# Experts' token rows sorted by indirect writes to memory, and one pool of five PSUM banks in the attention

## The chip, the cores and the metric

One core of a Trainium2 chip runs the whole program once. The metric is the device time of one execution in microseconds (us); a kernel's time is the median of its runs.

## What is computed

Two blocks on 256 tokens of width 1024, batch 1, in float32. The first block is two layers of a hybrid mixer and a SwiGLU feed-forward network. The second block takes its result as `x`, and a context `s` of another 256 tokens, through two layers that each end in a hierarchical mixture of experts; layer 0 mixes by pooling, layer 1 by attention from the tokens to context and tokens. The context is updated in layer 0 only, so layer 0's experts serve 512 tokens and layer 1's 256.

```python
x = first_block(x, ...)                      # 2 x (hybrid mixer, SwiGLU), final norm
for i in range(DEPTH):                       # second block: pool layer, attention layer
    a_lat = modulate(x, norm1_g[i], sh1, sc1)
    ...
    x = x + g1 * y_lat
    x = x + g2 * hier_moe(modulate(x, norm2_g[i], sh2, sc2), ...)
    if ctx_upd:                              # i == 0
        s = s + cg1 * y_ctx
        s = s + cg2 * hier_moe(modulate(s, norm2_g[i], csh2, csc2), ...)

def hier_moe(h, w_rg, b_rg, w_re, b_re, w_gate, w_up, w_down):
    # the best of 4 groups, its best 2 of 4 experts: 2 of 16 experts for a token
    gates = jnp.sum(jax.nn.one_hot(expert_id, N_EXPERTS) * e_w[..., None], axis=1)
    a = jnp.einsum('nd,edf->nef', hf, w_gate)          # 1024 -> 256
    b = jnp.einsum('nd,edf->nef', hf, w_up)
    hid = jax.nn.silu(a) * b * gates[..., None]
    return jnp.einsum('nef,efd->nd', hid, w_down)      # 256 -> 1024

def block(q_blk):                            # attention: 16 query heads, 4 key heads, 512 keys
    s = jnp.einsum('bqhgd,bkhd->bhgqk', q_blk, k_all)
    p = jax.nn.softmax(s, axis=-1)
    return jnp.einsum('bhgqk,bkhd->bqhgd', p, v_all)
```

## The kernel before

**Products.** A float32 product of the accuracy wanted is made of three fast ones (`fp32r`): each factor is split into a high part, which ScalarE writes (L422, L463), and a low rest, which VectorE or now and then GpSimd subtracts (L425, L465, L467); then hi x hi, hi x lo and lo x hi are added in one PSUM bank (L457 to L459). Weights come through SP's queue in loads of 1 MB into three buffers (`stg`, L406), and are split half by half into four pairs of buffers (`whi`, `wlo`), in layer 0's experts into three more (`xhi`, `xlo`: `wx`, every third split).

**Order.** The program is one long list of instructions with tiles from pools; the framework orders each engine's instructions ahead of time by a modelled timeline with the program's order as priority, takes buffers from the pools, and sets the semaphores. On the chip each engine, and each of the queues of SP and GpSimd, works its list in that fixed order.

**Stages in the order of time.** Mixer and feed-forward of layer 0, then of layer 1 of the first block. The second block's conditioning weights (`w_mod`, 80 loads of 0.5 MB through GpSimd's queue, used at L1268) run in between. While the second feed-forward network works, `context` (L1487) takes the context tokens through the pool layer, a step behind every few products, and writes their split rows to memory (`tokd`, L1527). Then `latent` (L1533) does the same for the tokens, and `experts0` (L1710) runs layer 0's experts for both. Then come the attention (`attn`), layer 1's tokens and experts, and the output.

**Sorting tokens for experts.** `tokens` (L1428) normalizes 256 tokens, makes the router's logits, and hands the rows on in four groups of 256 columns to a `sink`, which splits them (L1525, L1556). `route` (L1573) finds each token's two experts and its place among an expert's tokens (`pm`). In its second half it makes the row number `si` = 128 x expert + 64 x segment + place in a table of 16 x 128 rows; segment 0 are the tokens, 1 the context; if an expert has more than 64 tokens of a segment, another path is taken (`every_expert`). `quad_all` (L1757) does four experts at a time. First it builds a 0/1 matrix per segment (`places`, L1707) and multiplies the tokens' split rows with it, so that the tokens come out sorted by expert and transposed: 16 steps of four matmuls of 256 columns (L1768), each evacuated by ScalarE, every fourth by VectorE (L1770). Then, expert by expert, 24 matmuls of 512 columns with gate and up weights (L1781 to L1783), the activation (L1785 to L1787), two transposes (L1790) with a split, 12 matmuls with the down weights (L1798 to L1800), and a write of the 128 x 1024 result rows to `eb` (L1804). `gather` (L1733) fetches each token's two result rows by `si` with indirect DMAs, and `combine` weighs and adds them.

**Attention's banks.** `pools_b` (L1211) gives the attention two PSUM banks for projections (`mm`), three for scores (`ms`), two for transposes and others (`mx`), one for the outputs. In a step of `heads` two banks of scores are made (L2000, L2001), their maxima taken on VectorE (L2003), exponentials on ScalarE (L2007), the results transposed (L2011), evacuated, and multiplied with the values (L2016). The projections of the next heads are issued between.

Of the kernel before, what the change touches and what calls it, by code (L numbers as in the profile page):

```python
# [8 lines left out]
F32 = mybir.dt.float32  # L9
F32R = mybir.dt.float32r  # L10
# [9 lines left out]
KT = 8  # L20
# [243 lines left out]
class Halves:  # L264
# [3 lines left out]

    def __getitem__(self, key):
        return self.t[key[1] // 4][key[0], key[1] % 4]  # L270


class Prog:
# [926 lines left out]
    def pools_m(self, ctx):  # L1200

        P = self.pools(ctx)
        self.a1 = P("a1m", 4)
        self.pmm = P("pmm3", 3, space=PSUM)
        self.pm1 = P("pm1", 1, space=PSUM)
        self.pmx = P("pmx3", 4, space=PSUM)
        self.wx = P("wx", 3)
        self.b8 = P("b8", 3)
        self.b4 = P("b4", 2)

    def pools_b(self, ctx):  # L1211

        P = self.pools(ctx)
        self.a1 = P("a1b", 8)
        self.cb = P("cb", 1)
        self.a2 = P("a2d", 12)
        self.b8 = P("b8b", 8)
        self.b4 = P("b4b", 5)
        self.pmm = P("pmm4", 2, space=PSUM)
        self.pmx = P("pmx4", 2, space=PSUM)  # L1220
        self.pms = P("pms", 3, space=PSUM)
        self.pmo = P("pmo", 1, space=PSUM)
        self.c.update(self.consts("c2", self.cb))

# [81 lines left out]
            sink(kt, t, sh[:, kt:kt + 1])  # L1306

    def ms(self):
        return self.pms.tile([128, 512], F32, tag="ms", name="ms")

    def e8(self, dt=F32):
        return self.b8.tile([128, 8, 256], dt, tag="b8", name="b8")
# [115 lines left out]
    def tokens(self, x, l, seg, per, hold, SH, sink):  # L1428
# [44 lines left out]
        route = self.route(l, lg, seg, per)  # L1473
        self.R[l, seg] = next(route)
        yield
        for g, ps in enumerate(held):
            h = self.t2()
            for i in range(2):
                e = nc.vector.scalar_tensor_tensor(h[:, i], ps[:, i], r[:, i:i + 1], SH[:, g * 256:g * 256 + 256], op0=ALU.mult,
                                                   op1=ALU.add)  # L1480
                if seg == 0 and g + i == 0:
                    self.tc.keep_in_program_order(e)
            sink(g, h)
            yield
        next(route)

    def context(self):  # L1487

# [33 lines left out]

        def sink(g, ps):
            hi, lo = self.t2(F32R), self.t2(F32R)
            self.split_act(ps, hi, lo)  # L1525
            for w, z in enumerate((hi, lo)):
                nc.gpsimd.dma_start(self.tokd[w].rearrange("p (i n) -> p i n", i=2)[:, :, g * 256:g * 256 + 256], z)  # L1527
        yield from self.tokens(xc, 0, 1, 128, self.mx, SH, sink)
# [4 lines left out]
    def latent(self, x):  # L1533
# [19 lines left out]

        def sink(g, ps):
            s = slice(g * 256, g * 256 + 256)
            self.split_act(ps, self.tok[0][0][:, :, s], self.tok[0][1][:, :, s])  # L1556
        yield from self.tokens(x, 0, 0, 128, self.hold, SH, sink)

    def first(self, w, prio, tag):
# [150 lines left out]
    def experts0(self, R):  # L1710

        nc = self.nc
        for quad in range(4):
            self.quad_all(0, quad, self.tok, [self.places(r, quad) for r in R])
        with self.tc.If(self.count(R) > 64):
            Y = self.every_expert(0, self.tok, R)
            for seg, r in enumerate(R):
# [39 lines left out]
    def quad_all(self, l, quad, tok, Dt):  # L1757

        nc, a = self.nc, self.a
        X = [self.b8.tile([128, 4, 4, 2, 2, 64], F32R, tag="b8", name="xg") for hf in range(2)]  # L1760
        order = [(k, seg) for k in range(KT) for seg in range(2)]
        if quad == 0:
            order.sort(key=lambda o: -o[1])
        for n, (k, seg) in enumerate(order):
            ps = self.mm()
            for w in range(2):
                for t in range(2):
                    nc.tensor.matmul(ps[:, w], tok[seg][w][:, t, k * 128:k * 128 + 128],  # L1768
                                     Dt[seg][:, t].rearrange("p e s -> p (e s)"), start=t == 0, stop=t == 1)
            (nc.vector.tensor_copy if k % 4 == 3 else nc.scalar.copy)(  # L1770
                X[k // 4][:, k % 4, :, :, seg].rearrange("p e w s -> p w e s"), ps.rearrange("p w (e s) -> p w e s", e=4))
        for el in range(4):
            e = 4 * quad + el
            ps = self.mm().rearrange("p a b -> p (a b)")
            for c in range(2):
                for hf, (hi, lo) in enumerate(self.halves(a["moe"][l, e, c], 1024)):
                    for kk in range(2):
                        k = c * 4 + hf * 2 + kk
                        xh, xl = (X[c][:, hf * 2 + kk, el, w].rearrange("p g s -> p (g s)") for w in range(2))
                        s = slice(kk * 512, kk * 512 + 512)  # L1780
                        nc.tensor.matmul(ps, xh, hi[:, s], start=k == 0, stop=False)  # L1781
                        nc.tensor.matmul(ps, xh, lo[:, s], start=False, stop=False)
                        nc.tensor.matmul(ps, xl, hi[:, s], start=False, stop=k == KT - 1)  # L1783
# [18 lines left out]
            for q in range(2):  # L1802
                nc.scalar.copy(eo[:, q * 512:q * 512 + 512], po[q])
            (nc.sync if e == 15 else nc.gpsimd).dma_start(self.eb[e * 128:e * 128 + 128, :], eo)  # L1804

    def quad_few(self, l, quad, tok, D, gate, g2r, y):

# [329 lines left out]
    def rows_behind(self):  # L2137
# [4 lines left out]
        self.eb = self.dr.tile([2560, 1024], F32, name="eb")  # L2142
        for t in range(4):
            nc.gpsimd.dma_start(self.eb[2048 + t * 128:2176 + t * 128, :], z)

    def run(self):
        from contextlib import ExitStack
# [59 lines left out]
```

## Time and profile before

| | |
|---|---|
| Median of 3 runs | 1731.03 us (1719.16 to 1735.97) |
| The profiled execution | 1719.79 us, of it 1718.0 us from its first to its last instruction (the span) |
| Busy share of the span | TensorE 96%, VectorE 62%, ScalarE 47%, GpSimd 11% |
| DMA | 359.73 MB, on average 209 GB/s |
| Layer 0's experts | about 1184 to 1361 us |
| Attention's heads | about 1452 to 1542 us |

Times in the rows are us from the span's start. PE is TensorE's matmuls, PEld its weight loads (which overlap them), DVE VectorE, ACT ScalarE, POOL GpSimd, SPq the queue of SP. `out<-in` are the program's tiles; x is a count. The end of a matmul is modelled and consecutive ones overlap, so what a matmul costs is read from start to start. The DMA share is the mean busy share of the core's 16 DMA engines; the granted clock is TensorE's, as a share of the full one.

### The profile page before, as it was taken

Reading aid. Unit: us, or ns where it says so; the run is one execution under the profiler, and the core shown is the slowest. Engines: PE = TensorE matmul, PEld = TensorE weight load, DVE = VectorE, ACT = ScalarE, POOL = GpSimd, SP = SyncE. Lnnn points to the kernel's source line nnn. Section 1 sums busy time; section 2 is a strip of 40 time slices with the busy share of each in tenths; the row PEclk is TensorE's granted clock in tenths of the full one; section 3 lists DMA queues with packets and bytes.
Section 4 is the critical chain, followed back from the end, with each engine's and each line's share of the span. In section 5 each row is a group of like instructions: output and inputs, shape, how many; then the busy total and the mean of one; then the engine's idle time right before and its main releaser. Section 6 shows DMA issues by size and latency. Waiting matters only on the chain. (4 is left out here: it accounts for less than half of the span.)

```text
span 1718.0 us, 29620 instructions
## 1 busy us (share of the span) xinstructions
PE 1648.1 (96%) x12089; PEld 1403.2 (82%) x12089; DVE 1070.9 (62%) x1946; ACT 805.0 (47%) x1260; POOL 181.1 (11%) x281
## 2 busy tenths in 40 slices
PE   7999999999999999999999999998999799888997
PEld 6977889999999886788999999966777599566453
DVE  6863575666665595357677778457777567555222
ACT  4633264344444373235455554335777644552121
POOL 4311000110000230101002111020000201000000
PEclk9999999999999999999999999997999989998999
DMA  8574248875555665335555558565888744118991
GB/s 323 175 256 148 96 161 282 296 244 176 192 176 180 241 210 202 124 123 209 196 173 188 184 194 259 180 224 202 320 319 310 292 160 123 31 31 318 398 405 55
DMA packets 67276, 359.73 MB, mean 209 GB/s; under 512 B 8040, under 2 KB 13080, under 8 KB 34744
## 3 DMA queue, kind: packets, MB, share of 16 engines
q1 hardware_dynamic: 41280, 279.86, 45.0%
q0 software_dynamic: 25632, 77.47, 13.4%
q8 instruction: 100, 1.64, 0.4%
q10 hardware_dynamic: 216, 0.37, 0.1%
q14 instruction: 48, 0.39, 0.1%
HBM read 339.76 MB, written 14.71 MB: 206 GB/s over the span
## 5 line engine op out<-in xcount | busy, mean ns | idle before, releaser
L425 DVE TENSOR_TENSOR wlo<-stg,whi 128x1024 fp32r<-128x1024 f32 (+1 forms) x379 | 462.3, 1226 | 286.9 <-ACT whi L422 279.6
L422 ACT ACTIVATE whi<-stg 128x1024 fp32r<-128x1024 f32 (+1 forms) x383 | 402.2, 1056 | 475.8 <-PE mm L458 289.2
L457 PE MATMUL mm<-hh,whi 128*128 128x256 f32 x1408 | 408.3, 290 | 10.9 <-ACT whi L422 9.7
L458 PE MATMUL mm<-hl,whi 128*128 128x256 f32 x1408 | 403.1, 286 | 0.0
L459 PE MATMUL mm<-hh,wlo 128*128 128x256 f32 x1408 | 402.4, 286 | 0.6 <-DVE wlo L425 0.5
L457 PEld LDWEIGHTS mm<-hh,whi 128*128 128x128 f32 x1408 | 271.9, 193 | 22.7 <-ACT whi L422 9.7
L459 PEld LDWEIGHTS mm<-hh,wlo 128*128 128x128 f32 x1408 | 272.0, 193 | 3.9 <-issue 2.5
L458 PEld LDWEIGHTS mm<-hl,whi 128*128 128x128 f32 x1408 | 272.1, 193 | 3.3 <-issue 2.9
L411 POOL DMA_DIRECT2D st<-in_w_mod x80 | 42.6, 534 | 416.1 <-PE ad L1268 371.8
L494 POOL TENSOR_TENSOR a<-a,a 128x256 f32<-128x256 f32 x30 | 27.5, 918 | 312.1 <-ACT a L492 310.9
L614 PE MATMUL mm<-wlo,hh 128*128 128x512 f32 (+1 forms) x160 | 60.0, 375 | 0.0
L615 PE MATMUL mm<-whi,hl 128*128 128x512 f32 (+1 forms) x160 | 60.0, 375 | 0.0
L613 PE MATMUL mm<-whi,hh 128*128 128x512 f32 (+1 forms) x160 | 59.5, 378 | 0.0
L1268 PE MATMUL ad<-st,sc 128*32 128x256 f32 x640 | 51.8, 389 | 2.9 <-DMA st<-in_w_mod 2.9
L457 PE MATMUL mm<-lg,whi 128*128 128x256 f32 x192 | 54.5, 284 | 0.0
L457 PE MATMUL mx<-lg,whi 128*128 128x256 f32 x192 | 54.4, 285 | 0.0
L458 PE MATMUL mm<-lg,whi 128*128 128x256 f32 x192 | 54.3, 283 | 0.0
L459 PE MATMUL mm<-lg,wlo 128*128 128x256 f32 x192 | 54.3, 283 | 0.0
L458 PE MATMUL mx<-lg,whi 128*128 128x256 f32 x192 | 54.2, 283 | 0.0
L459 PE MATMUL mx<-lg,wlo 128*128 128x256 f32 x192 | 54.1, 283 | 0.0
L1862 DVE TENSOR_TENSOR eo<-mx,g2r 128x512 f32<-128x512 f32 x16 | 11.0, 690 | 66.1 <-PE mx L1857 65.8
L425 DVE TENSOR_TENSOR xlo<-stg,xhi 128x1024 fp32r<-128x1024 f32 x31 | 37.8, 1220 | 13.9 <-ACT xhi L422 13.9
(600 smaller groups left out, 3597.1 us busy)
## 6 DMA issues: line engine op xcount, KB each, us to landing
stg<-in_moe SPq DMA_DIRECT2D x57, 1024.0 KB
stg<-in_w_gu SPq DMA_DIRECT2D x44, 1024.0 KB
stg<-in_w_fm SPq DMA_DIRECT2D x43, 1024.0 KB
st<-in_w_mod POOLq DMA_DIRECT2D x80, 512.0 KB, 5.5
w<-in_moe SPq DMA_DIRECT2D x27, 1024.0 KB
stg<-in_w_dn SPq DMA_DIRECT2D x22, 1024.0 KB
stg<-in_w_tm SPq DMA_DIRECT2D x16, 1024.0 KB
stg<-in_w_br SPq DMA_DIRECT2D x12, 1024.0 KB
```

The lines of the kernel that those rows point to most:

```text
L411: self.nc.gpsimd.dma_start(t, src)
L422: nc.scalar.activation(hi[:, :n], t, AF.Copy)
L425: (nc.gpsimd if pool else nc.vector).tensor_sub(lo[:, :n], t, hi[:, :n])
L457: nc.tensor.matmul(out, hi, xh, start=first and k == 0, stop=False)
L458: nc.tensor.matmul(out, hi, xl, start=False, stop=False)
L459: nc.tensor.matmul(out, lo, xh, start=False, stop=last and k == n - 1)
L494: self.adder.tensor_add(sq[0][1], sq[0][1], s)
L613: nc.tensor.matmul(ps[i], xh[:, ts], hi[:, s], start=first, stop=False)
L614: nc.tensor.matmul(ps[i], xh[:, ts], lo[:, s], start=False, stop=False)
L615: nc.tensor.matmul(ps[i], xl[:, ts], hi[:, s], start=False, stop=last)
L1268: nc.tensor.matmul(ps[32 * n:32 * n + 32, :256], self.sc[:, 2 * q + hf], ws[hf][:, n * 256:n * 256 + 256], start=hf == first, stop=hf == last)
L1862: nc.vector.tensor_mul(eo, po[q], g2r[:, q * 512:q * 512 + 512])
```

## The change

- `tokens` gets, for layer 0, two row tiles of 128 x 1024 (`rowsof`) instead of four tiles of 128 x 2 x 256, so that each token's whole row lies in one partition. Behind the last group four indirect DMAs on GpSimd's queue write the rows (128 at a time, for each of a token's two experts) to the rows `si` of a new table `xs` of 2048 x 1024 in memory. For the context the second half of `route` comes ahead of the rows and not behind them. The two sinks split the rows in halves of 256 columns instead of 512.
- `quad_all` keeps the matmul dispatch for quad 0. For quads 1 to 3 a new `slots` loads, for each expert, its 128 rows from `xs` through SP's queue into one of two buffers (`xr`), transposes them in eight steps of 128 columns into two banks, and splits each bank (512 columns) once on ScalarE and VectorE. The 0/1 matrices of these quads are not built.
- `rows_behind` also clears rows 512 to 2047 of `xs`: 12 writes of 0.5 MB through GpSimd's queue.
- The third `wx` buffer pair makes room for the `xr` buffers.
- In the attention the banks for projections and scores become one pool of five under one tag.

```diff
+class Pieces(list):
+
+    def __getitem__(self, key):
+        return list.__getitem__(self, key[1])
...
-        self.wx = P("wx", 3)
+        self.wx = P("wx", 2)
+        self.xr = P("xr", 2)
...
-        self.pmm = P("pmm4", 2, space=PSUM)
+        self.pmm = P("pmm4", 5, space=PSUM)
         self.pmx = P("pmx4", 2, space=PSUM)
-        self.pms = P("pms", 3, space=PSUM)
...
     def ms(self):
-        return self.pms.tile([128, 512], F32, tag="ms", name="ms")
+        return self.pmm.tile([128, 512], F32, tag="mm", name="ms")
...
         self.R[l, seg] = next(route)
         yield
+        if seg:
+            next(route)
+        H = l == 0 and [self.rowsof(seg) for i in range(2)]
         for g, ps in enumerate(held):
-            h = self.t2()
+            h = Pieces([z[:, g * 256:g * 256 + 256] for z in H]) if H else self.t2()
...
-        next(route)
+        if not seg:
+            next(route)
+        if H:
+
+            for i in range(2):
+                for k in range(2):
+                    nc.gpsimd.indirect_dma_start(
+                        out=self.xs[:, :], out_offset=bass.IndirectOffsetOnAxis(ap=self.R[l, seg]["si"][:, k, i, 0:1], axis=0),
+                        in_=H[i], in_offset=None)
+
+    def rowsof(self, seg):
+        return self.t4().rearrange("p a b -> p (a b)") if seg else self.ca.tile([128, 1024], F32, tag="row", name="row", bufs=2)
...
-            self.split_act(ps, hi, lo)
+            for i in range(2):
+                self.split_act(ps[:, i], hi[:, i], lo[:, i])
...
-            self.split_act(ps, self.tok[0][0][:, :, s], self.tok[0][1][:, :, s])
+            for i in range(2):
+                self.split_act(ps[:, i], self.tok[0][0][:, i, s], self.tok[0][1][:, i, s])
...
-            self.quad_all(0, quad, self.tok, [self.places(r, quad) for r in R])
+            self.quad_all(0, quad, self.tok, [] if quad else [self.places(r, quad) for r in R])
...
+        if quad:
+            pieces = self.slots(quad)
+        else:
+            X = [self.b8.tile([128, 4, 4, 2, 2, 64], F32R, tag="b8", name="xg") for hf in range(2)]
...
         for el in range(4):
             e = 4 * quad + el
+            piece = next(pieces)
...
-                        xh, xl = (X[c][:, hf * 2 + kk, el, w].rearrange("p g s -> p (g s)") for w in range(2))
+                        xh, xl = (piece(k, w) for w in range(2))
...
+    def slots(self, quad):
+
+        nc = self.nc
+        for el in range(4):
+            e = 4 * quad + el
+            if el % 2 == 0:
+                X = self.b8.tile([128, 2, KT, 2, 128], F32R, tag="b8", name="xg")
+            r = self.xr.tile([128, 1024], F32, tag="xr", name="xr")
+            nc.sync.dma_start(r, self.xs[e * 128:e * 128 + 128, :])
+            for q in range(2):
+                ps = self.mm().rearrange("p a (k s) -> p (a k) s", k=2)
+                for k in range(4):
+                    nc.tensor.transpose(ps[:, k], r[:, (4 * q + k) * 128:(4 * q + k) * 128 + 128], self.idf)
+                x = X[:, el % 2, 4 * q:4 * q + 4]
+                self.split_act(ps, x[:, :, 0], x[:, :, 1])
+            yield lambda k, w, x=X[:, el % 2]: x[:, k, w]
...
+        self.xs = self.dr.tile([2048, 1024], F32, name="xs")
+        for t in range(4, 16):
+            nc.gpsimd.dma_start(self.xs[t * 128:t * 128 + 128, :], z)
```

## Rows read from the trace of the kernel before

**Rows 1.** The page: span, and busy time of TensorE with instructions.

```profile
span 1718.0 us, 29620 instructions
PE 1648.1 (96%) x12089; PEld 1403.2 (82%) x12089; DVE 1070.9 (62%) x1946; ACT 805.0 (47%) x1260; POOL 181.1 (11%) x281
```

**Rows 2.** Windows: length, busy us of five engines, clock, DMA share, GB/s.

```profile
1180.00:1190.00 10.00, 9.78 (x60) 8.63 (x59) 7.95 (x10) 8.52 (x12) 0.00 (x0) 1.00 0.27 95
1190.00:1352.00 162.00, 151.86 (x743) 122.95 (x742) 125.28 (x146) 123.54 (x180) 7.46 (x14) 1.00 0.89 324
1240.00:1250.00 10.00, 9.32 (x43) 6.96 (x42) 8.09 (x10) 8.62 (x12) 0.53 (x1) 1.00 0.93 345
1325.00:1330.00 5.00, 3.86 (x16) 2.67 (x15) 4.31 (x6) 4.04 (x5) 0.53 (x1) 1.00 0.63 206
1600.00:1650.00 50.00, 50.00 (x260) 26.32 (x260) 12.18 (x25) 11.14 (x23) 0.00 (x0) 1.00 1.01 406
```

**Rows 3.** Timeline of TensorE: transposes of experts 11, 12 and 13.

```profile
1315.64 0.38 PE L1790 MATMUL mx<-idf,a 128*128 128x128 f32 x2
1333.74 0.38 PE L1790 MATMUL mx<-idf,a 128*128 128x128 f32 x2
1341.09 0.38 PE L1790 MATMUL mx<-idf,a 128*128 128x128 f32 x2
```

**Rows 4.** Waits, 1184-1361 us: total, times, longest; ScalarE, load queue.

```profile
ACT xhi L422 <- DMA stg<-in_moe: 22.9, 9, 4.1
SPq L406 <- DVE wlo L425: 54.9, 15, 9.2
```

**Rows 5.** Groups of 1184 to 1361 us: busy us, mean ns, idle before.

```profile
L1768 PE MATMUL mm<-Dt,tok 128*128 128x256 f32 x198 | 30.3, 290 | 2.3 <-ACT xg L1770 2.3
L1770 ACT CAST xg<-mm 128x512 fp32r<-128x512 f32 x37 | 21.2, 607 | 0.3 <-PE mm L1783 0.3
L1770 DVE CAST xg<-mm 128x512 fp32r<-128x512 f32 x13 | 8.9, 686 | 2.4 <-PE mm L1768 2.4
L1707 DVE TENSOR_TENSOR Dt<-cst_cg,pm 128x512 fp32r<-128x512 f32 x5 | 3.4, 681 | 0.0
```

**Rows 6.** Timeline of TensorE: start, length, one merged run each.

```profile
1222.54 0.38 PE L1790 MATMUL mx<-idf,a 128*128 128x128 f32 x2
1222.68 1.84 PE L1768 MATMUL mm<-Dt,tok 128*128 128x256 f32 x12
1225.28 1.11 PE L1768 MATMUL mm<-Dt,tok 128*128 128x256 f32 x8
1226.23 0.63 PE L1800 MATMUL mx<-xhi,a 128*128 128x512 f32 x2
```

**Rows 7.** Groups: subtractions of 512 columns (1100-1184 us), 256 (1184-1361 us).

```profile
L465 DVE TENSOR_TENSOR tok<-a,tok 128x512 fp32r<-128x512 f32 x4 | 2.6, 681 | 0.0
L467 DVE SCALAR_TENSOR_TENSOR a<-mx,a 128x256 fp32r<-128x256 f32 x16 | 6.7, 417 | 1.4 <-ACT a L463 1.4
```

**Rows 8.** The indirect gathers: issue on GpSimd, and landing.

```profile
L1733 POOL DMA_INDIRECT rows<-eb,si x8: 945/958/1963, 1365.5 to 1374.8; - x8
DMA to landing us min/median/max: 7.9/8.0/10.0
```

**Rows 9.** Timeline of GpSimd: idle time in brackets.

```profile
349.21 0.95 POOL L494 TENSOR_TENSOR a<-a,a 128x256 f32<-128x256 f32 x1 [25.12 <-ACT a L492]
1115.03 2.39 POOL L425 TENSOR_TENSOR wlo<-stg,whi 128x1024 fp32r<-128x1024 f32 x1 [67.14 <-ACT whi L422]
```

**Rows 10.** Window of the clears, and their DMA issues with median landing.

```profile
324.00:364.00 40.00, 40.00 (x347) 39.11 (x346) 32.36 (x40) 20.49 (x31) 6.01 (x9) 1.00 0.68 246
eb<-a POOLq DMA_DIRECT2D x4, 512.0 KB, 11.1
```

**Rows 11.** Attention's heads: window, and TensorE's longest wait in it.

```profile
1452.00:1542.00 90.00, 80.48 (x479) 53.47 (x478) 50.75 (x110) 52.50 (x108) 6.29 (x8) 0.96 0.15 44
PE mx L2011 <- ACT a L2007: 6.2, 6, 1.6
```

More of the change, by code (lines that the diff above doesn't have):

```diff
@@ L1759, in quad_all @@
         nc, a = self.nc, self.a
[L1760 to L1771, printed above, removed]
+        if quad:
+            pieces = self.slots(quad)
+        else:
+            X = [self.b8.tile([128, 4, 4, 2, 2, 64], F32R, tag="b8", name="xg") for hf in range(2)]
+            order = sorted([(k, seg) for k in range(KT) for seg in range(2)], key=lambda o: -o[1])
+            for n, (k, seg) in enumerate(order):
+                ps = self.mm()
+                for w in range(2):
+                    for t in range(2):
+                        nc.tensor.matmul(ps[:, w], tok[seg][w][:, t, k * 128:k * 128 + 128],
+                                         Dt[seg][:, t].rearrange("p e s -> p (e s)"), start=t == 0, stop=t == 1)
+                (nc.vector.tensor_copy if k % 4 == 3 else nc.scalar.copy)(
+                    X[k // 4][:, k % 4, :, :, seg].rearrange("p e w s -> p w e s"), ps.rearrange("p w (e s) -> p w e s", e=4))
+            pieces = (lambda k, w, el=el: X[k // 4][:, k % 4, el, w].rearrange("p g s -> p (g s)") for el in range(4))
         for el in range(4):
             e = 4 * quad + el
+            piece = next(pieces)
             ps = self.mm().rearrange("p a b -> p (a b)")
```

## Prediction

> **What bounds it now.** The page's busy table comes first [rows 1]: in a span of 1718.0 us TensorE is counted busy for 96%. That looks like a kernel in which every matmul taken out is time gained, and the change takes matmuls out. A share over the whole span says nothing of one stage, so the second view is the windows over the stage that the change rewrites, layer 0's sixteen experts [rows 2]. From 1190 to 1352 us TensorE is busy 151.9 of 162 us, and the DMA engines at the same time 89%, moving 324 GB/s: 52.5 MB. Two resources are near their end together there, and the reader should keep both in sight. Third, the order in time [rows 3]: the transposes of the expert before a quad's boundary and of the one behind it are 18.1 us apart (1315.64 to 1333.74), those of two experts inside the quad 7.35 us. One of three is shown; the others take 17.3 and 18.8 us. The extra time is the dispatch: the sixteen products of token rows with 0/1 matrices that sort the next quad's tokens. While TensorE works on it, no split weight is used up, the split buffers and then the three weight buffers stay full, and the loads stop: behind the boundary, from 1325 to 1330 us, the DMA share is 0.63 although weights are still to come [rows 2]. Fourth, the waits [rows 4]: in this stage ScalarE's splits wait for weights that have not landed (22.9 us at one of the two buffer kinds), and the load queue waits mostly for the split that gives a buffer back. So the stage goes back and forth between a dispatch that stops the loads and loads that are then late.
>
> **What the dispatch costs and what takes its place.** Quads 1 to 3 lose 3 x 64 = 192 matmuls of 256 columns (198 in [rows 5], which counts the last six of quad 0). Eight of them in a row take from 1225.28 to 1226.23 us, 0.119 us each [rows 6]: 22.8 us of TensorE. Added are 12 experts x 8 transposes of 128 columns. The expert's own pair of transposes takes from 1222.54 to 1222.68, 0.07 us each [rows 6]; 0.12 us, a dispatch matmul of twice the columns, is the other end. I take 0.09: 8.6 us (6.7 to 11.5). TensorE's need falls by 14.2 us, to 137.7 us in that stretch.
>
> ScalarE loses 36 evacuations of 0.607 us (21.8 us) and gets 24 splits of the same 512 columns (14.6 us): 7 us less. VectorE loses 12 of 0.686 us and six comparisons of 0.681 us that built the 0/1 matrices (12.3 us) and gets 24 subtractions of 0.681 us (16.3 us) [rows 5, 7]: 4 us more. Both were under 80% busy in the stretch (123.5 and 125.3 of 162 us [rows 2]), so neither sets its end.
>
> The DMA engines get more to do: 12 reads of 0.524 MB, 6.3 MB. Two of the row buffers can be filled before 1190 us, where only 95 GB/s move [rows 2], so 52.5 + 6.3 - 1.0 = 57.8 MB are left for the stretch. The rate decides. 324 GB/s at a share of 0.89 are 364 GB/s at a full one. 345 GB/s is what a single stretch without a pause reached (1240 to 1250 us, share 0.93), and 406 GB/s the layer-1 experts' stage, where hardly anything is split [rows 2]. At 364 the bytes need 159 us, at 345 they need 168, at 406 they need 142 and TensorE with the 10 us of gaps that it has now (148 us) would be the limit. I take 364, the row of the same weights on the same queue with the same splits beside them, and another microsecond from the smoother order: the stage gets **4 us shorter**; ends 14 shorter and 6 longer. The 14 us that TensorE gives back are for the most part taken up by the new reads.
>
> A rule of the Trainium skill reads otherwise. SBUF — State Buffer, Summary: rules for kernel authors, says to reckon with about 358 GB/s between HBM and SBUF. By it the bytes would need 161 us and the stage would gain 1 us; the 406 GB/s of layer 1 lie above it, so this trace does not bear it out as a ceiling.
>
> **The split buffers.** One pair of the seven split buffers goes (wx from 3 to 2) to make room for the rows. Six halves are one whole expert, so a step ahead remains. From nothing to a doubling of what TensorE idles in the stretch now (10 us); I take **+1 us**, since the dispatch that emptied and filled these buffers in turns is gone.
>
> **The scatters.** Eight indirect writes replace the sorting matmuls. GpSimd spent 0.96 us (1.96 at most) on one indirect gather and it landed in 8.0 us, 10.0 at most [rows 8]. The context's four come while the feed-forward layer runs: GpSimd then stood idle for 67 us [rows 9]. The latent's four come right before the stage, 4 x 1.0 + 10 = 14 us, and their rows are first read for expert 4, behind four experts of at least 7.35 us each [rows 3]. Both cost nothing as long as the first read of rows does not stand in SP's queue ahead of weights while it waits for the scatter; that would cost the weights behind it a few us once. Taken at 0, the end +3.
>
> The tokens' split goes from four pieces of 512 columns to eight of 256. On VectorE that is 8 x 0.417 in place of 4 x 0.681 us [rows 7], +0.6 us on the path to the first dispatch; the context's is covered by the feed-forward layer. **+0.5 us**.
>
> **The clearing of the sorted rows** is 12 writes of 0.5 MB behind the four that are there, at the start of layer 0's feed-forward. GpSimd's issues cost it 6.4 us out of an idle time of 25 us [rows 9]. The engines are at 0.68 from 324 to 364 us [rows 10], so 0.32 x 40 us x 364 GB/s = 4.7 MB fit in and 1.6 MB, 4.4 us of transfers, are pushed past it, ahead of conditioning weights on the same GpSimd queue which TensorE uses in order. The four writes took 11.1 us to land [rows 10]. Ends 0 and +5; I take **+1 us**.
>
> **The attention's banks.** The heads' stretch, 1452 to 1542 us, has TensorE busy for 80.5 of 90 us, and the named wait is that of the transposes for ScalarE's exponentials, 6.2 us [rows 11]. Scores are made in pairs, and three banks hold one pair and a half, so the second score of the next step must wait until a bank of this step has been exponentiated. Five hold two pairs and leave one for a projection. What can be won ends at the idle 9.5 us. It could cost as well: a projection that comes while four banks hold scores has one bank instead of two of its own, and TensorE's order is fixed, so what stands behind a product that lacks its bank waits too; no row prices it, and I bound it by half of the wait that is there, +3. I take somewhat less than two thirds of the named wait: **-4 us** (-9.5 to +3).
>
> **Sum.** -4 + 1 + 0 + 0.5 + 1 - 4 = -5.5 us on 1718.0, so 1712.5 us of span; 1.8 us lie around it (the profiled execution took 1719.8). The median of the runs, 1731.0, stands 11.2 us above that execution, and I take the same distance for the changed kernel: 1712.5 + 1.8 + 11.2 = **1725.5 us**, written as 1725.
>
> **Rivals.**
> - **Faster: the loads keep up.** With the dispatch gone nothing stops the loads, and they run at layer 1's 406 GB/s. Then TensorE's 148 us set the stretch, the stage gains 14 us, and the time is 1715 us. For it: 406 GB/s at a share of 1.01. Against: in that stage VectorE works 24% of the time, here 77% [rows 2]. HBM Reference in the Trainium skill, Specifications (TRN2), gives about 425 GB/s for a core that streams alone; that speaks for this rival, and no stretch of the experts' stage here shows it.
> - **Slower: the buffers, not the engines, set the rate.** If three weight buffers and six split pairs turn over no faster than now, the loads stay at the stage's 324 GB/s. 57.8 MB then need 178 us, 16 us more than the 162: with the other terms 1745 us. It decides from 357 GB/s downwards, where 57.8 MB need over 162 us. For it: the load queue's waits are for splits [rows 4]. Against: the largest cause that kept the buffers full goes, and the row reads have buffers of their own.
> - **A draw: reads eat the whole gain.** At the unbroken 345 GB/s the stretch is 6 us longer, and if the banks bring nothing too (softmax is a chain through three engines, and more banks shorten none of its steps), the sum is +6 + 1 + 0.5 + 1 = +8.5: 1739 us.
>
> **Chances and range.** Forecast 0.42, loads keep up 0.26, draw 0.18, buffers set the rate 0.14. About 1% (17 us) is what a measurement of this kernel can tell from no change. Faster by more means below 1714: half of the keep-up case (0.13) and a third of the forecast's spread, where the banks bring their whole 9.5 us (0.14). Slower by more means above 1748: the better part of the buffer case (0.09) and a third of the draw, with the clears and the split buffers at their upper ends (0.06). That gives 0.27, 0.58, 0.15. The range runs from the keep-up case with the banks' upper end (1709) a little down, to the buffer case: 1706 to 1745. The forecast's own range is 1714 to 1735.
>
> **What would show it.** In the experts' stretch: no 18 us steps at quad boundaries but even ones near 11 us; TensorE down by about 14 us busy and idle more; the DMA share at 0.95 or more without the dips to 0.6, near 360 GB/s; ScalarE's waits for weights longer than now. If the share stays at 0.89 with the load queue waiting for splits, the buffer case is right; if GB/s go over 395 and TensorE is above 95% busy, the keep-up case. In the heads' stretch the wait for the exponentials should fall from 6.2 to about 2 us. At 361 to 384 us TensorE should show no wait for conditioning weights beyond a few us; a longer one would make the clears the mis-sized term, and a wait of the load queue for the scatter ahead of expert 4 would make it the scatters.

## The result, and the profile after

The changed kernel takes 1747.3 us (median of 4 runs, 1743.4 to 1750.7) against 1726.8 us of the kernel before, measured beside it (median of 4 runs): a ratio of 1.0111, 95% interval 1.0075 to 1.0147. A second set of runs (after_again, below) gave 1.0150 (1.0115 to 1.0185). The profiled execution's span is 1747.5 us against 1718.0 [rows 1].

The profile page of the kernel after, span and busy times:

```profile
span 1747.5 us, 29487 instructions
PE 1646.5 (94%) x11993; PEld 1397.1 (80%) x11993; DVE 1076.4 (62%) x1960; ACT 802.2 (46%) x1256; POOL 196.8 (11%) x301
```

TensorE is busy as long as before, with 96 matmuls fewer by the profile page's count, in a span 29.5 us longer. (Line numbers in a view are those of its own kernel: L1791 is L1768 of the kernel before.) Its timeline at the start of the experts has the largest piece: one idle stretch of 18.87 us, in brackets with what ended it, inside quad 0's dispatch, ahead of 48 of its 64 matmuls.

```profile
1192.58 8.17 PE L1791 MATMUL mm<-Dt,tok 128*128 128x256 f32 x48 [18.87 <-ACT xg L1793]
```

ScalarE and VectorE, which had to evacuate that dispatch, waited in turn, for the transfers that scatter the latent's rows:

```profile
1191.88 0.69 DVE L1793 CAST xg<-mm 128x512 fp32r<-128x512 f32 x1 [9.12 <-DMA xs<-row,si]
...
1191.94 1.56 ACT L1793 CAST xg<-mm 128x512 fp32r<-128x512 f32 x3 [10.44 <-DMA xs<-row,si]
```

And GpSimd issued the four scatters one at a time, each behind the landing of the one before:

```profile
1172.92 1.03 POOL L1500 DMA_INDIRECT xs<-row,si  x1 [1.52 <-DVE si L1651]
1181.30 0.98 POOL L1500 DMA_INDIRECT xs<-row,si  x1 [7.36 <-DMA xs<-row,si]
1184.90 0.96 POOL L1500 DMA_INDIRECT xs<-row,si  x1 [2.62 <-DMA xs<-row,si]
1188.48 0.96 POOL L1500 DMA_INDIRECT xs<-row,si  x1 [2.62 <-DMA xs<-row,si]
```

Nothing in the computation ties quad 0's sorted tokens to the scatters. Memory does: the allocation puts the latent's two row tiles at bytes 204,768 to 212,960 of each partition, in a pool (`ca`) that begins at 196,576, and lays the pool of the sorted tiles (`b8`), 171,744 to 220,896, over them. The evacuations that waited write the first sorted tile, at 171,744 to 188,128, which shares no byte with the rows; only the second, at 204,512 to 220,896, does. So the wait goes with the whole pool: its first writers wait until the last scatter has read its rows.

The queue of SP, which the prediction had named, waited too. The first row read stood there for 19.6 us, with the weights behind it:

```profile
SPq L1839 <- DMA xs<-row,si: 19.6, 1, 19.6
```

Windows of the kernel after (columns as in [rows 2]): the clears' stretch, and the experts' with the same distances to the first gate and the last down matmul as there.

```profile
324.00:364.00 40.00, 40.00 (x346) 39.11 (x346) 30.19 (x38) 20.46 (x30) 10.53 (x20) 1.00 1.01 405
...
1206.00:1378.00 172.00, 149.59 (x667) 116.57 (x666) 131.63 (x156) 120.59 (x169) 7.55 (x14) 0.97 0.91 335
```

The clears fill the idle 32% of the engines [rows 10] and TensorE stays busy for all 40 us. In the experts' stretch 57.6 MB move at 335 GB/s, where 52.5 MB moved at 324 before [rows 2]: 172 us for 162. The waits there, 1200 to 1387 us (total, times, longest), beside [rows 4]:

```profile
ACT whi L428 <- DMA stg<-in_moe: 14.9, 13, 4.3
...
PE mx L1815 <- DVE a L1812: 10.9, 6, 2.7
PE mm L1806 <- ACT whi L428: 9.5, 5, 3.1
ACT xhi L428 <- DMA stg<-in_moe: 9.2, 5, 3.0
...
SPq L412 <- DVE wlo L431: 65.2, 20, 11.4
...
SPq L1839 <- PE mm L1843: 22.6, 8, 4.7
```

The last is the row reads, waiting for a row buffer with the weights behind them; the second is new too, TensorE waiting for an expert's activation, which the dispatch matmuls used to cover. ScalarE's waits for weights are 24.1 us at both kinds of buffer, where they were 35.0 before (22.9 in [rows 4] and 12.1 at the other kind).

### The profile page after: what moved, and what is told of

Its sections match the earlier page's. It is cut to its first block, busy times and chain, and to the rows that moved or that the text cites. A ratio compares the mean times of both kernels' runs of the same rounds, so it can differ in the third digit from the quotient of the medians.

```text
span 1747.5 us, 29487 instructions
## 1 busy us (share of the span) xinstructions
PE 1646.5 (94%) x11993; PEld 1397.1 (80%) x11993; DVE 1076.4 (62%) x1960; ACT 802.2 (46%) x1256; POOL 196.8 (11%) x301
## 5 line engine op out<-in xcount | busy, mean ns | idle before, releaser
L1904 DVE TENSOR_TENSOR eo<-mx,g2r 128x512 f32<-128x512 f32 x16 | 11.1, 692 | 66.1 <-PE mx L1899 65.8
```

Of the source, the lines that this page charges most:

```text
L1904: nc.vector.tensor_mul(eo, po[q], g2r[:, q * 512:q * 512 + 512])
```

## The experiments

The table gives each kernel's median in us and its ratio to before on the same chip, and from the views of single lines **a**, the time from the start of the last conditioning matmul to that of the first gate matmul, and **b**, from there to the start of the last down matmul. Before stood between 1721.8 and 1723.8 us in the sets of the experiments. The last conditioning matmul starts between 1161 and 1175 us in these executions, a shift that a and b leave out. They come from one execution of each kernel: after and after_again, the same kernel, differ by 5.4 us in b, so a smaller difference in a single trace shows little.

| kernel | us | ratio (95%) | a | b | a+b |
|---|---|---|---|---|---|
| before | - | 1 | 17.9 | 175.8 | 193.7 |
| after | 1747.3 | 1.0111 (1.0075-1.0147) | 36.6 | 184.9 | 221.5 |
| row_late | 1743.7 | 1.0109 (1.0072-1.0145) | 15.8 | 193.9 | 209.7 |
| row_late_gp | 1743.1 | 1.0102 (1.0055-1.0150) | 15.9 | 201.1 | 217.0 |
| row_late_one | 1730.7 | 1.0039 (1.0008-1.0069) | 15.8 | 182.4 | 198.2 |
| five_alone | 1729.3 | 1.0043 (1.0014-1.0073) | 17.9 | 176.8 | 194.7 |
| row_clear | 1738.3 | 1.0085 (1.0059-1.0110) | 16.1 | 192.6 | 208.7 |
| row_clear_banks23 | 1734.2 | 1.0075 (1.0048-1.0103) | 17.4 | 184.0 | 201.4 |
| reads_alone | 1727.9 | 1.0042 (1.0015-1.0069) | 17.6 | 186.8 | 204.4 |
| wx2_alone | 1719.1 | 0.9976 (0.9957-0.9996) | 18.1 | 175.2 | 193.3 |
| scatters_alone | 1733.0 | 1.0056 (1.0034-1.0077) | 16.0 | 190.5 | 206.5 |
| row_clear_23_one | 1725.0 | 0.9994 (0.9969-1.0019) | 16.1 | 182.3 | 198.4 |
| wx2_stage4 | 1717.1 | 0.9962 (0.9942-0.9982) | 18.1 | 169.0 | 187.1 |
| scatters_apart | 1728.4 | 1.0035 (1.0014-1.0056) | 17.4 | 178.7 | 196.1 |
| rows_apart | 1730.9 | 1.0045 (1.0022-1.0069) | 16.3 | 185.3 | 201.6 |
| rows_apart_one | 1720.0 | 0.9981 (0.9962-1.0000) | 16.2 | 178.6 | 194.8 |
| rows_apart_gp | 1729.2 | 1.0035 (1.0011-1.0059) | 16.3 | 183.0 | 199.3 |
| apart_five | 1729.8 | 1.0028 (1.0008-1.0048) | 16.2 | 182.6 | 198.8 |
| after_again | 1747.8 | 1.0150 (1.0115-1.0185) | 36.6 | 179.5 | 216.1 |
| wx1_stage5 | 1758.0 | 1.0200 (1.0169-1.0231) | 18.2 | 204.8 | 223.0 |

**The first four: move the memory, move the queue, leave reads out, the banks alone.**

```
 # row_late, in pools_m
-wx, xr, b8, b4
+b8, b4, xr, wx
 # row_late_gp, besides: nc.gpsimd.dma_start(r, self.xs[...]) for nc.sync
 # row_late_one, besides: only "if el == 0:" reads a row tile
 # five_alone: before, with pmm4 of 5 banks and pms gone
```

> The changed kernel with the order of four pools turned round (b8, b4, xr, wx for wx, xr, b8, b4), so that the memory of the latent's two row tiles is given next to the result tiles (b4) and the row buffers (xr) and no longer to quad 0's sorted tiles (xg in b8). Theory (18 us of the loss is the wait of quad 0's evacuations for memory that the scatters still read): TensorE no longer idles 18.9 us ahead of quad 0's products, the first gate matmul comes at about 1182 us and not at 1200.6, and the time falls by 15 to 19 us against the changed kernel, to about 1729 us. Rival (the scatters themselves hold the stage up, by their traffic or by the queue they stand in): the first gate matmul stays near 1200 and the time within 4 us of the changed kernel's.

> As row_late, and the twelve reads of sorted rows go through GpSimd's queue instead of SP's. Theory A (the experts' stretch, 9 us longer than before, is bound by the bytes): the same as row_late within 3 us. Theory B (a row read that waits for its buffer stands ahead of weight loads in SP's queue, 22.6 us in all): 5 to 9 us faster than row_late, and SP's waits for the row buffers are gone. Theory C (one split buffer pair fewer): the same as row_late.

> As row_late, but only the first of a quad's four row blocks is read, and all four experts of the quad are given it: nine of twelve reads (4.7 MB) are left out, so experts 5 to 7, 9 to 11 and 13 to 15 compute with another expert's rows. Theory A (bytes): 4.7 MB at 335 to 368 GB/s are 13 to 14 us of transfers; the stretch gets 8 to 12 us shorter than in row_late. Theory B (row reads ahead of weights in SP's queue): 5 to 8 us shorter here and in row_late_gp alike. Theory C (split buffers): within 3 us of row_late.

> The kernel before with the attention's pool of five banks alone. Forecast's step: 4 us faster than the kernel before (0 to 9.5), the wait of the transposes for the exponentials falls from 6.2 to about 2 us. Rival (softmax is a chain through three engines, and more banks shorten none of its steps): within 2 us of the kernel before; the wait moves to the products with the values.

The stall in quad 0's dispatch went (a: 36.6 to 15.8 us), and the kernel was hardly faster where 15 to 19 us were expected, because other tiles now lay on the rows. Timelines of TensorE and ScalarE in row_late:

```profile
1210.27 1.22 PE L1823 MATMUL mx<-xhi,a 128*128 128x512 f32 x2 [12.05 <-ACT xhi L428]
...
1209.16 2.00 ACT L428 ACTIVATE xhi<-stg 128x1024 fp32r<-128x1024 f32 x2 [4.47 <-DMA xs<-row,si]
```

The split buffers begin at byte 212,704 there, 256 bytes inside the second row tile. Reading from the other queue won nothing. Leaving out 4.7 MB of reads (and with them the right rows) won 11.5 us of a+b, of which 4.9 us are a shorter stall (7.16 us for 12.05). five_alone missed both of its cases: it is 0.43% slower, where the forecast had 4 us less and the rival no more than 2 us either way.

**Rows clear of both, and two parts alone.** row_clear puts a gap of 256 bytes ahead of the split buffers; row_clear_banks23 also takes the pool of five back.

```
 # row_clear
+self.gap = P("gap", 1); nc.gpsimd.memset(self.gap.tile([128, 64], F32, name="gap"), 0.0)
 self.wx = P("wx", 2)
 # reads_alone: before with wx 2 and xr 2, and for quads 1 to 3, ahead of each expert
+nc.sync.dma_start(self.xr.tile([128, 1024], F32, tag="xr", name="xr"), self.eb[2048 + e % 4 * 128:2176 + e % 4 * 128, :])
 # wx2_alone: before with wx 2
```

> The changed kernel with its SBUF laid out so that the latent's two row tiles share bytes with the row-read buffers and the output tiles alone, and no byte with the sorted tiles or with the split buffers (those start 256 bytes further up). Theory M (both stalls at the experts' start, 18.9 us before the gate matmuls in the changed kernel and 12.1 us behind the first of them in row_late, are waits for the memory that the scatters read): no TensorE wait over 3 us between 1180 and 1215 ends with the scatters or behind them, last conditioning to first gate matmul 16 to 18 us, first gate to last down matmul about 182 us (row_late: 193.9), and the kernel at 1729 to 1734. Rival S (the scatters themselves hold up the loads on the DMA engines, whatever the memory): the first gate to last down stretch stays at 190 us or more and the kernel at 1740 to 1746.

> row_clear with the attention's banks as before the change (two for projections, three for scores). If the pool of five is worth the 4 us that the prediction gave it, this is 3 to 5 us slower than row_clear, from the scores' first matmul to the last pv matmul. If five_alone was right (about 4 to 5 us slower behind the gather), it is 3 to 6 us faster than row_clear, and at 1724 to 1729 level with the kernel before.

> The kernel before with two split buffers for three, and twelve reads of 0.5 MB, one ahead of the weights of each expert from 4 to 15, into two buffers that nothing reads (rows of zeros from memory; computes the same). No scatter, no transposes of rows, no splits, and the dispatch matmuls stay. Theory A (the experts' stretch is set by the bytes, at 52.5 MB plus 6.3 MB): first gate to last down matmul 8 to 13 us longer than in wx2_alone, the DMA rate of the stretch up by under 10 GB/s. Rival C (the stretch has 11% of idle DMA time that takes the reads, and the changed kernel's 9 us come from TensorE's order, where no dispatch matmuls cover the activation, and from the waits for splits): within 2 us of wx2_alone, the DMA share up to 0.97 or more.

> The kernel before with two split buffers for three in the experts' stretch, nothing else. The prediction put this at +1 us. If the buffers set the rate of the weights' stream: first gate to last down matmul 4 us or more longer, with longer waits of SP's queue for the VectorE's low parts (54.9 us before). If not: within 2 us.

wx2_alone came out as "not the rate", and 2.7 us better rather than worse. reads_alone did what theory A said of the time: 6.3 MB that nobody uses cost 11.6 us of b, and 8.9 us of the median; the rate rose by 13 GB/s, where under 10 were expected. Windows of b in wx2_alone, then in reads_alone:

```profile
1186.10:1361.30 175.20, 165.59 (x801) 136.59 (x800) 135.74 (x157) 132.25 (x191) 8.00 (x15) 0.98 0.82 303
```

```profile
1181.10:1367.90 186.80, 169.62 (x801) 136.64 (x801) 136.31 (x158) 134.11 (x192) 7.99 (x15) 0.97 0.83 316
```

The share hardly moves, 0.82 to 0.83. At 364 GB/s, a share of 1, the reads need 17.3 us, so the idle 18% took in a third of them; the rest of it was no room. row_clear fits neither theory whole: its a is that of M, its b of 192.6 us that of S, its median lies between the two, and TensorE has no wait of 3 us or more at the experts' start. row_clear_banks23 is 4.1 us faster, which the runs cannot tell from nothing (the intervals overlap), and not level with before. In b, row_clear runs the same sequence of instructions as row_clear_banks23 and took 8.6 us longer; TensorE was busy 163.0 and 157.5 us on it. (The execution of row_clear_banks23 that was profiled, 1725.6 us, is the fastest of its six.) Their timelines behind the same wait, row_clear first:

```profile
1227.05 0.69 PE L1817 MATMUL mx<-idf,a 128*128 128x128 f32 x2 [5.59 <-DVE a L1814]
...
1231.79 0.63 PE L1827 MATMUL mx<-whi,a 128*128 128x512 f32 x1
1232.21 0.63 PE L1825 MATMUL mx<-whi,a 128*128 128x512 f32 x1
1232.64 0.63 PE L1826 MATMUL mx<-wlo,a 128*128 128x512 f32 x1
```

```profile
1219.83 0.44 PE L1818 MATMUL mx<-idf,a 128*128 128x128 f32 x2 [3.80 <-DVE a L1815]
...
1224.12 0.39 PE L1828 MATMUL mx<-whi,a 128*128 128x512 f32 x1
1224.34 0.39 PE L1826 MATMUL mx<-whi,a 128*128 128x512 f32 x1
1224.57 0.39 PE L1827 MATMUL mx<-wlo,a 128*128 128x512 f32 x1
```

Starts 0.43 us apart are the lower of the clock's two levels (1.2 GHz; the granted clock reads 0.50 from 1229.5 to 1233 us in row_clear), 0.23 us the higher (2.4 GHz; 1.00 from 1224.3 to 1230 us in row_clear_banks23). The first still ran at the lower 5 us behind the gap, the second no longer after 4.3. Here a gap cost more than its length.

**Sorting without its use, chain or bytes, one load buffer more.**

```
 # scatters_alone: row_clear_banks23, quads 1 to 3 dispatched as before the change, xs never read
 # row_clear_23_one: row_clear_banks23 with "if el == 0:" ahead of the row read
 # wx2_stage4: before with wx 2, and in load():
+fourth = self.wx and self.nld % 4 == 0
+t = (self.sx if fourth else self.stg).tile([128, 2048], F32, ...)
```

> Sorting without its use: the tokens' halves, the clears and the eight scatters stay as in row_clear, with the rows' memory apart from what the experts' first steps write, but the sorted rows are never read, and all four groups of experts are dispatched by matmuls as before the change (two split buffers, attention's banks as before). The prediction put the scatters at 0 (end +3). Theory A: once their memory is apart they cost nothing, so last conditioning to first gate matmul 16 to 18 us, first gate to last down matmul within 2 us of wx2_alone's 175.2, the kernel within 3 us of wx2_alone (0.997 to 1.000 of before). Rival S (the scatters' 2 MB in packets of one row, and GpSimd's time for them, hold up the loads at the experts' start): first gate to last down 179 us or more and the kernel 4 us or more above wx2_alone, which would explain why row_clear_banks23 stands above reads_alone.

> row_clear_banks23 with one row read for every four: the experts of a group read the first one's tile again, so nine of twelve reads (4.7 MB) are left out, and with them the right rows; every transpose, split and matmul stays. Theory A (TensorE's saving is real, but the stretch goes by bytes): first gate to last down matmul 170 to 175 us, below before's 175.8, and the kernel at 0.995 to 1.000 of before. Rival C (the activation chain that no dispatch matmul covers any more, and the clock that falls in its gaps, set the stretch): 180 us or more, within 4 us of row_clear_banks23's 184.0, and the kernel at 1.004 or more.

> The kernel before with two split buffers for three in the experts' stretch, and the 8 KB that this frees given to a fourth buffer for the weights' loads, which every fourth load of that stretch takes. If the loads' queue, which waits 55 us for low parts that free its buffers, sets the rate: DMA rate up from 302 GB/s between first gate and last down matmul, that stretch 3 to 8 us shorter than wx2_alone's 175.2 (TensorE's busy 165 us is the floor), and the kernel at 0.993 to 0.997 of before. If TensorE sets it: within 2 us of wx2_alone.

scatters_alone spoke for S, and against "cleared memory": b was 15.3 us longer than in wx2_alone. ScalarE's timeline shows why:

```profile
1212.76 1.07 ACT L1830 COPY b<-mx 128x512 f32<-128x512 f32 x2 [8.32 <-DMA xs<-row,si]
```

That is the first expert's output, copied to bytes 196,320 to 200,416, where no row ever lay. But another tile of the row tiles' pool lay there, and the release waits for the whole pool, as in the kernel after. So none of the kernels so far had its rows really apart. In row_clear and row_clear_banks23 ScalarE shows no such wait; in row_clear_23_one it waited 7.4 us, so that this run told little of chain or bytes.

**Rows in a pool of their own**, at the same addresses:

```
 # scatters_apart = scatters_alone +, rows_apart = row_clear_banks23 +, apart_five = row_clear +
+self.rowp = P("rowp", 2, side="right")
 self.ca = P("ca", 1, side="right")
 # rowsof: self.rowp.tile(...) for self.ca.tile(...)
```

> scatters_alone with the latent's row tiles in a pool of their own, at the same addresses: there the first expert's output copy on ScalarE waited 8.3 us for the last scatter, since its buffer takes memory of the pool that held the row tiles (other tiles of that pool). Again the sorted rows are never read and all experts are dispatched by matmuls. Theory M (the waits for the scattered rows' memory were all that the scatters cost): first gate to last down matmul within 3 us of wx2_alone's 175.2, the kernel at 0.996 to 1.001 of before. Rival S (the scatters' traffic or GpSimd's time itself): 180 us or more, and the kernel at 1.003 or more.

> row_clear_banks23 with the latent's row tiles in a pool of their own, so that of the experts' first steps only the first row reads wait for the scatters. Theory A (bytes: reads_alone was 11.6 us longer in the stretch than wx2_alone, and TensorE's saving takes 0 to 5 us off that): first gate to last down matmul 180 to 187 us, the kernel at 1.001 to 1.005 of before. Rival M (memory alone, the reads are hidden): 172 to 178 us and 0.994 to 0.999.

> rows_apart with one row read for every four: the experts of a group read the first one's tile again, so nine of twelve reads (4.7 MB) and with them the right rows are left out; transposes, splits and matmuls stay. Theory A: first gate to last down matmul 170 to 176 us, the kernel at 0.993 to 0.998 of before, some 8 us below rows_apart. Rival C (the uncovered activation chain and the clock in its gaps): 180 us or more, within 4 us of rows_apart.

> rows_apart with the row reads issued by GpSimd for SyncE, so that no weights stand behind a row read that waits for the last scatter or for a free buffer. Theory Q (SyncE's queue: the first row read waits up to 8.6 us for the scatters with the weights behind it): 4 to 8 us shorter between first gate and last down matmul than rows_apart, and the kernel at 0.996 to 1.000 of before. Theory A alone: within 3 us of rows_apart, as row_late_gp was no faster than row_late.

With only the pool changed scatters_apart's b fell by 11.8 us to 178.7, as theory M has it in the main, though 3.5 us above wx2_alone where 3 were allowed; the kernel, at 1.0035 of before, stands where rival S had put it, since it loses more behind the experts (below). rows_apart fell where theory A said, at 185.3, inside 180 to 187; rows_apart_one, at 178.6, lies between theory A's 170 to 176 and rival C's 180, but the medians of the two are 11.0 us apart, where C allowed 4. The queue is not the cause: rows_apart_gp is 2.3 us shorter in b and 1.7 us in the median, within what the runs can tell. TensorE's longest waits between 1184 and 1372 us, in rows_apart and then in rows_apart_one, bear on the dispute between the bytes and the uncovered activation chain:

```profile
PE mx L1819 <- DVE a L1816: 14.6, 9, 2.4
PE mm L1810 <- ACT whi L428: 5.8, 4, 2.7
PE mm L1811 <- DVE wlo L431: 2.4, 5, 0.8
```

```profile
PE mm L1810 <- ACT whi L428: 6.4, 7, 1.5
PE mm L1811 <- DVE wlo L431: 5.8, 10, 0.8
```

With nine reads gone the wait for the activation is no longer among them (2.9 us are left), though the chain is as uncovered as before. So the uncovered chain is what late bytes look like: with the next expert's weights or rows there, its matmuls cover the chain as the dispatch did.

**The sum on one chip, and the load buffers once more.**

> rows_apart with the attention's pool of five: the whole changed kernel, its computation and its transfers unchanged, with no wait left for the memory of the scattered rows but that of the row reads. Theory M+A: against after_again on the same chip 8 to 14 us faster (18.9 us of stall ahead of the first gate matmul gone; the stretch as in rows_apart, 183 to 187 us, against 184.9), so 1.001 to 1.006 of before. If the pool of five costs what five_alone's median says (0.4%), it is 3 to 7 us above rows_apart; if nothing, level with it.

> The changed kernel once more, on the same chip as apart_five, so that the two are compared by one set of runs: 1.0075 to 1.015 of before, and again one TensorE wait of 16 to 20 us for the sorted tiles' evacuation between the last conditioning and the first gate matmul.

> The kernel before with one split buffer of the third kind instead of three in the experts' stretch, and the 16 KB given to a fourth and fifth buffer for the weights' loads. If staging sets the rate of the stretch (wx2_stage4: 169.0 us against wx2_alone's 175.2): 163 to 168 us and 0.992 to 0.996 of before; TensorE's busy time of 162 to 165 us is the floor. If one split buffer of that kind is too few: waits of ScalarE for the low parts' readers, the stretch at 170 us or more, and the kernel at 0.996 or above.

apart_five is the whole changed kernel, its work and transfers as they are, with the rows' memory apart: 1729.8 against 1747.8 us on the same chip. The two differ in where their tiles lie in SBUF, and in one small write into the gap. **18.0 of the 24.0 us that the change costs there are the wait for memory** (a falls from 36.6 to 16.2 us), more than the 8 to 14 expected, and 6.0 us remain. On the pool of five apart_five is 1.1 us below rows_apart and row_clear 4.1 above row_clear_banks23, both within the intervals; only five_alone, 0.14 to 0.73% above before, is clear of them. The stretch behind the gather, down to the normalization of the combined rows, took 45 to 53 us in all these kernels; it holds most of five_alone's loss and of what scatters_apart loses over its b. It is longer where the granted clock is lower. Windows of it, before and then in five_alone:

```profile
1365.50:1410.70 45.20, 40.02 (x313) 38.28 (x311) 24.59 (x68) 20.67 (x49) 10.01 (x11) 0.87 0.52 209
...
1364.90:1415.50 50.60, 44.68 (x326) 42.17 (x325) 25.98 (x69) 22.21 (x50) 10.31 (x11) 0.79 0.49 189
```

It took 44.6 us at a clock of 0.90 in wx2_alone, 49.2 at 0.80 in scatters_apart, and 52.7 at 0.77 in apart_five. What lowered the clock there no run shows.

wx2_stage4 is the fastest kernel here, 0.38% below before; its b is 6.2 us shorter than wx2_alone's, with TensorE's clock at 1.00 for 0.98. In the whole kernel the intervals of the two overlap, so that the fourth load buffer helps is shown by that one execution alone:

```profile
1192.80:1361.80 169.00, 161.62 (x801) 133.81 (x800) 137.52 (x158) 136.40 (x192) 7.99 (x15) 1.00 0.83 310
```

wx1_stage5 missed by far, and in the way its second case says: with one pair left, ScalarE waits for that pair's readers, and the load queue for its low part (125.7 us, 27 times), so b is 204.8 us. Its waits from 1181 us on:

```profile
ACT xhi L424 <- PE mx L1803: 22.8, 15, 3.0
ACT xhi L424 <- PE mm L1786: 12.1, 15, 1.7
```

## Why the prediction was wrong, step by step

**The scatters at 0 (end +3) are the step that failed.** The prediction gave them one condition, SP's queue. That queue did wait, 19.6 us in the kernel after, the sign that the prediction had named; but where only this wait is left, rows_apart_gp puts its price at some 2 us. The condition that held 18 us was never asked: who writes next to the memory that the scatter is still reading? The row tiles were taken from a pool that closes right behind them, and a pool of the next stage lies on its bytes. The duration was mis-sized as well: 4 x 1.0 + 10 = 14 us took the four as overlapping. They were issued one behind the landing of the other, 19 us from the first issue to the end of the wait in the kernel after, and 37 us (1175.69 to 1212.76) in scatters_alone, where loads run beside them.

**The experts' stretch, -4 us, came out at about +5.** Even without the stall the forecast fails, in its direction too: the change then costs 6.0 us, where 5.5 fewer were forecast. apart_five, without the memory wait, has a+b of 198.8 against 193.7. By parts: reads +11.1 (reads_alone), scatters +2.8 (scatters_apart), both against wx2_alone's 193.3; that makes 207.2, and rows_apart has 201.6, so the dispatch that went is worth 5.6 us by this sum of single executions, about what two of one kernel differ by. The mechanism was right in the main, bytes in the place of TensorE's work; two terms were mis-sized. The bytes were not 57.8 but 59.8 MB in apart_five's window cut like [rows 2]: the first row reads wait for the scatters and none is ahead, which is 1.0 of the 2.0 MB, and the rest was not traced. And 364 GB/s became 354, since a share of 1.0 was never reached:

```profile
1192.30:1361.10 168.80, 147.04 (x654) 115.26 (x653) 132.44 (x157) 121.58 (x170) 10.14 (x17) 0.96 0.93 354
```

At a full share the 354 would be 381, so the step from a share to a rate at 1.0 does not hold from kernel to kernel. TensorE's need, put at 137.7 us, reads 147.0, at a clock of 0.96 where it was 1.00. Of the rivals, the draw (345 GB/s, the stretch 6 us longer) describes the part that is not the stall. The buffer case gave 1745 us, close to the result, but that is luck: 18 us of it are the stall. Its signs came in part: in the kernel after, the share was 0.91 and the load queue waited 65.2 us for low parts, 54.9 before. No run gave the changed kernel another load buffer, so how its stretch divides between bytes and buffers stays open. The 354 GB/s at a share of 0.93 lie next to the 358 of the Trainium skill (SBUF — State Buffer, Summary: rules for kernel authors), and the 405 GB/s of the clears' window above it: the traces bear it out as a price for that window, not as a ceiling.

**The banks, -4 us: nothing won.** The wait that the step went by did go. TensorE's waits in the heads of the kernel after, 1479.7 to 1576 us, beside [rows 11]:

```profile
PE ms L2042 <- DMA QQ<-QQ: 4.2, 1, 4.2
PE po L2058 <- ACT b L2054: 0.6, 1, 0.6
```

The scores were finished 8 us earlier in the stretch, but from the first score to the last product with the values it takes 95.7 us, 94.2 before; in the seven other traces with the pool of five it takes 94.3 to 95.9. The step took a wait of TensorE for the stretch's length. More banks let scores run ahead; exponentials, transposes and products behind them still follow one another, as the draw had put it.

**What held, and what did not.** The clears show no cost in the trace (+1 was taken): the window moved 6.4 MB more than before, as much as the clears are, where 4.7 had been reckoned to fit, and TensorE shows no wait at 361 to 384 us; no run leaves them out. The tokens' split, +0.5: it lies in a, which is 16.2 us in apart_five and 17.9 before. The split buffers, +1: wx2_alone is 2.7 us faster. From expert to expert it took 11.3 us on average in the kernel after, without the 18 us at the quads' boundaries (13.2, 12.9 and 8.3), but the steps are not even: they run from 5.7 to 17.1 us. ScalarE's waits for weights, forecast as longer, are shorter.

## What to carry to other kernels

When a transfer out of SBUF replaces computation, ask of its source tile as of any other who writes to that memory next, and how long the transfer really holds them; a pool that closes behind it hands the wait to whatever opens there, and another order of the pools with an own pool for the late reader gave 18 us back. In a stage where two resources are near their end, work taken from one and bytes given to the other are weighed against each other by a run of the bytes alone. Before moving a few KB from one kind of buffer to another, find which queue waits for which buffer: 8 KB moved from splits to loads made b 6 us shorter in the execution profiled, the next 8 KB 36 us longer.

## What the hardware showed unexpectedly

From the issue of one indirect write of 128 rows of 4 KB to that of the next, which waits for its landing, it took 8.4 us in the kernel after while 312 GB/s moved beside it (1173 to 1181 us), and 3.6 us at 150 GB/s (1181 to 1192 us). In scatters_alone, with the weights' stream of 308 GB/s, GpSimd waited 7 to 9 us for each; a chain of four took 19 to 37 us. After idle gaps of 5.6 and 3.8 us the same run of matmuls stayed at the clock's lower level for some 6 and 4 us. And an idle share of the DMA engines was no room: at a share of 0.82, 6.3 MB more still cost two thirds of the time that they need alone.
